# A transformer block with mLSTM, windowed attention and PEER experts: the front half reordered around its modulation, with gated late loads

## The chip, the cores and the metric

The program runs on one core of a Trainium2 chip. The metric is the device time of one execution in microseconds (us); where several executions are shown, their median counts.

## The reference, cut to what is computed

```python
sh1, sc1, g1, sh2, sc2, g2 = split(silu(c) @ w_ada + b_ada, 6)      # 6 x 1024, also for the context
h_lat = rms(x) * norm_mix_g * (1 + sc1) + sh1                      # x: 512 tokens x 1024
h_ctx = ...                                                        # the same for 256 context tokens
p = h @ w_in          # mLSTM q, k, v, o and gates; attention q (8 heads), k, v (2 heads); 2 x 1024 merge gates
m = mlstm(...)        # 4 heads of 128, chunks of 128, forwards and backwards, rms, times sigmoid(o)
a = window_attention(...)  # blocks of 128 queries, keys of 3 blocks and 256 of context, sink, rope
x = x + g1 * ((sigmoid(gm) * (m @ w_bm) + sigmoid(ga) * (a @ w_ba)) @ w_out)
x = x + g2 * peer(rms(x) * norm_ffn_g * (1 + sc2) + sh2)
# peer: 8 heads, 2 x 128 sub keys, top 16 of 16384 experts; gelu(u . h), weighted sum of v; u, v: 16384 x 1024
```

All in float32.

## The kernel before, in words

A product in nearly full precision is made of three matmuls in the `float32r` type (`mm3`): an operand is split into a high part `hi` (an ACT copy) and a low part `lo` (VectorE, DVE, or GpSimd, POOL, subtracts the high part). This is `split`. Weights come in tiles of 512 KB (`wraw`, four buffers), their parts are `whi` and `wlo` (three buffers each). TensorE is called PE, the engine whose queue issues most DMAs SP.

The front, up to 583 us, has these stages. The first half of the modulation's columns that the front needs comes from PE out of `w_ada0`; the rest from DVE `dot`s over a transposed `w_ada`: `late_mod` inside the first projection, `adas` for the 32 columns (`mod[:, 16:48]`) that only the merge and PEER read. `silu` prepares the vector for these dots. `modulated` tokens `xT`, scaled by the root mean square (`rms_rows`), are split to `hhi`, `hlo` and projected with `w_in`. Then come the four mLSTM heads, a preparation of attention's q and k (root mean square, rope, stacking), attention in four blocks `n` of 128 queries with 4, 5, 5 and 4 key blocks, each key block being eight transposes (`PE.transpose(pp...)`), two copies out of PSUM into `pTs` and two products; then a merge with `w_bm` and `w_ba`, `w_out`, and the norm ahead of PEER.

Twenty gate projections (`gate_proj`, 24 matmuls each: four `sigo`, sixteen merge gates, the latter stored in `sgd` and read back in the merge) depend on `hhi` alone. The code writes them after attention, but a list scheduler orders the front's instructions for each engine, and each engine runs its instructions in that order; so gates stand in mLSTM and attention where PE would have nothing else. `ahead(n)` loads tiles of the expert matrix U, makes their low parts and stores them in memory (`lows`); PEER loads them there instead of subtracting. Buffers are reused in a ring, so a load waits until the last reader of its buffer is done. PEER, from 583 us, is written out in an order of its own: query tiles, then streams of U and V tiles, with selection and gathers between.

Before, the loads of `adas` have no other condition than their two buffers (`wada2`), and the scheduler issues them during the projections:

```python
w = wk.tile([128, D], F32, name="wada2", bufs=2)
nc.sync.dma_start(w, A["w_adaT"][j])
dot(w, 0, mod[:, j:j + 1])
```

Of the kernel before, what the change touches and what calls it, by code (L numbers as in the profile page):

```python
# [11 lines left out]
F32 = mybir.dt.float32  # L12
# [16 lines left out]
NH, DH = 4, 128  # L29
# [6 lines left out]
P0, P1 = 10, N1 + 2  # L36


def body(ctx, tc, A, out):
# [147 lines left out]
    for k in range(8):  # L187
        for c in range(2):
            PE.matmul(pm[0:2, c], cc[:, 1, k], wa0[k][:, c], start=(k == 0), stop=(k == 7))
    mrow = [wb([2, 512], F32, "mrow") for _ in range(2)]  # L190
# [6 lines left out]
    pr = rms_rows(acc, T)  # L197
    accc = wk.tile([128, T], F32, name="accc", tag="R", bufs=2)[:, 0:TC]
    for k in range(8):
        square(xcT, k, accc, TC)  # L200
    rc = rms_rows(accc, TC)
    for k in range(8):
        V.tensor_tensor(out=xT[:, k], in0=xT[:, k], in1=pr, op=ALU.mult)
# [8 lines left out]
    for k in range(8):  # L212
        V.tensor_tensor(out=xcT[:, k], in0=xcT[:, k], in1=rc, op=ALU.mult)
# [1179 lines left out]
```

## Time and profile before

| what | value |
|---|---|
| median of three executions | 1848.27 us (1845.07 to 1852.2) |
| the profiled execution | 1850.52 us, its span 1848.7 us |
| mean granted PE clock in it | 0.973 |
| PE, DVE, ACT, POOL busy | 94%, 77%, 41%, 29% of the span |
| bytes moved by DMA | 483.52 MB |
| first mLSTM matmul | 196.3 us |
| first attention score | 311.4 us |
| first merge matmul | 470.0 us |
| first PEER matmul | 583.1 us |

The profile is of one execution; busy shares are averages over stages with different limits, so what an edit is worth has to be read from its own stage.

### The profile page before, as it was taken

The page shows a single profiled execution, that of the slowest core. Times are in us where ns is not written, and L with a number is a line of the kernel's source. Part 1 is how long each engine was busy: PE and PEld are TensorE (multiplying, and loading weights), DVE is VectorE, ACT ScalarE, POOL GpSimd, SP SyncE. Part 2 cuts the span into 40 slices and gives each one's busy share as a digit, 9 for nine tenths or more (in the row PEclk, how much of TensorE's full clock was granted, in tenths as well). Part 3 has the DMA queues.
Part 4 walks back from the last instruction along what each step waited for, and adds up shares of the span by engine and source line. Part 5 has one row for each costly group of instructions (what it writes and reads, how often), then busy time and mean ns, then how long its engine had stood idle before and what let it go on. Part 6 is the DMA issues. An engine that isn't in the chain of part 4 may idle for free.

```text
span 1848.7 us, 25030 instructions
## 1 busy us (share of the span) xinstructions
PE 1741.6 (94%) x9079; PEld 1487.9 (80%) x9079; DVE 1420.8 (77%) x2727; ACT 758.4 (41%) x1126; POOL 529.6 (29%) x422
## 2 busy tenths in 40 slices
PE   6989986998997999999999999999999999999998
PEld 2877875664776889988888999999999999988886
DVE  5858788644654999988828888888888898986665
ACT  5431464655445334544443333333333333333332
POOL 0130154220202554000015454544454454520000
PEclk7999998999998999999989999999999999999999
DMA  8586324545696325699999999999999999987662
GB/s 344 164 282 188 126 86 159 172 145 191 198 305 191 106 90 175 222 323 319 331 310 387 339 352 342 357 344 334 362 327 355 352 331 360 341 335 275 223 213 107
DMA packets 213741, 483.52 MB, mean 262 GB/s; under 512 B 15600, under 2 KB 107248, under 8 KB 212720
## 3 DMA queue, kind: packets, MB, share of 16 engines
q1 hardware_dynamic: 125632, 313.86, 48.1%
q0 software_dynamic: 36864, 134.23, 19.9%
q10 hardware_dynamic: 51120, 33.82, 5.8%
q8 instruction: 71, 1.16, 0.3%
q14 instruction: 54, 0.44, 0.1%
HBM read 419.73 MB, written 62.13 MB: 261 GB/s over the span
## 4 chain that ended last, share of the span: by engine, by line
PE 57%; DMA 8%; DVE 5%; ACT 3%; issue 1%; SPq 1%; ACTq 0%; POOL 0%; DVEq 0%
PE pa L177 9%; PE pa L178 9%; PE pa L176 9%; PE pu L176 9%; PE pu L178 9%; PE pu L177 9%; DMA Gd<-stg 5%; ACT stg L996 1%; DMA wraw<-in_w_out 1%; PE pg L852 1%; PE pg L989 1%; DMA gath<-in_u,idx 1%; DVE pos1h L910 1%; DMA xr<-in_xT 1%; DVE pos1h L899 1%
## 5 line engine op out<-in xcount | busy, mean ns | idle before, releaser
L176 PE MATMUL pu<-h2hi,whi 128*128 128x384 f32 (+1 forms) x1152 | 404.0, 351 | 11.9 <-ACT St L1100 8.3
L178 PE MATMUL pu<-h2lo,whi 128*128 128x384 f32 (+1 forms) x1152 | 396.9, 345 | 0.0
L177 PE MATMUL pu<-h2hi,wlo 128*128 128x384 f32 (+1 forms) x1152 | 396.5, 344 | 0.0
L767 DVE TENSOR_TENSOR wlo<-wraw,whi 128x1024 fp32r<-128x1024 f32 x210 | 256.7, 1223 | 104.4 <-ACT whi L756 102.8
L177 PE MATMUL pa<-whi,wl 128*128 128x512 f32 x768 | 301.3, 392 | 1.5 <-DVE wl L1116 1.4
L176 PE MATMUL pa<-whi,wh 128*128 128x512 f32 x768 | 299.6, 390 | 2.1 <-ACT wh L1112 2.0
L178 PE MATMUL pa<-wlo,wh 128*128 128x512 f32 x768 | 301.1, 392 | 0.0
L756 ACT ACTIVATE whi<-wraw 128x1024 fp32r<-128x1024 f32 x272 | 286.6, 1054 | 27.1 <-PE pa L177 11.8
L1043 POOL DMA_INDIRECT gath<-in_u,idx x128 | 165.1, 1290 | 415.4 <-DMA Sd<-St 241.3
L176 PEld LDWEIGHTS pu<-h2hi,whi 128*128 128x128 f32 x1152 | 219.4, 190 | 22.3 <-ACT St L1100 10.1
L177 PEld LDWEIGHTS pu<-h2hi,wlo 128*128 128x128 f32 x1152 | 219.3, 190 | 7.8
L178 PEld LDWEIGHTS pu<-h2lo,whi 128*128 128x128 f32 x1152 | 218.6, 190 | 5.7 <-DVE h2lo L52 0.6
L1043 POOL DMA_INDIRECT gath<-in_v,idx x128 | 162.0, 1266 | 180.7 <-DVE tokh L1075 164.9
L176 PEld LDWEIGHTS pa<-whi,wh 128*128 128x128 f32 x768 | 144.7, 188 | 31.5 <-ACT wh L1112 3.2
L177 PEld LDWEIGHTS pa<-whi,wl 128*128 128x128 f32 x768 | 144.5, 188 | 31.5 <-DVE wl L1116 2.9
L178 PEld LDWEIGHTS pa<-wlo,wh 128*128 128x128 f32 x768 | 144.4, 188 | 30.0
L1075 DVE SCALAR_TENSOR_TENSOR tokh<-gath,gw,tokh 128x1024 f32<-128x1024 f32 x127 | 162.7, 1281 | 0.6
L1067 DVE CUSTOM_DVE_ANT_0 gath<-gath,tokh 128x1024 f32<-128x1024 f32 x128 | 155.0, 1221 | 5.5 <-DMA gath<-in_u,idx 5.5
L52 POOL TENSOR_TENSOR wlo<-wraw,whi 128x1024 fp32r<-128x1024 f32 (+1 forms) x28 | 71.0, 2538 | 291.1 <-ACT whi L51 232.6
L1112 ACT ACTIVATE wh<-act 128x384 fp32r<-128x384 f32 x84 | 44.2, 526 | 256.8 <-DVE act L1108 254.7
L1100 ACT ACTIVATE act<-pu 128x384 f32<-128x384 f32 x84 | 41.3, 492 | 188.6 <-PE pu L178 188.6
L177 PE MATMUL ps<-hhi,wlo 128*128 128x512 f32 x224 | 93.6, 418 | 11.6 <-POOL wlo L52 11.6
(348 smaller groups left out, 2816.4 us busy)
## 6 DMA issues: line engine op xcount, KB each, us to landing
wraw<-in_uT SPq DMA_DIRECT2D x128, 512.0 KB
wraw<-in_v SPq DMA_DIRECT2D x128, 512.0 KB
Gd<-stg ACTq DMA_DIRECT2D x24, 1024.0 KB
Gt<-Gd SPq DMA_DIRECT2D x32, 768.0 KB
wraw<-in_w_in SPq DMA_DIRECT2D x40, 512.0 KB
sraw<-in_uT SPq DMA_DIRECT2D x36, 512.0 KB
lows<-sraw SPq DMA_DIRECT2D x36, 512.0 KB
wlo<-lows SPq DMA_DIRECT2D x36, 512.0 KB
```

Source lines behind the costliest of these rows:

```text
L52: (eng or V).tensor_tensor(out=lo, in0=src, in1=hi.bitcast(F32), op=ALU.subtract)
L176: PE.matmul(p, sh, mh, start=first, stop=False)
L177: PE.matmul(p, sl, mh, start=False, stop=False)
L178: PE.matmul(p, sh, ml, start=False, stop=last)
L756: S.activation(his[j], raws[j], AF.Copy)
L767: (G if pool else V).tensor_tensor(out=los[j], in0=raws.pop(j), in1=his[j].bitcast(F32), op=ALU.subtract)
L852: PE.matmul(p[:, b], qss[hp][:, b * 128:b * 128 + 128], subk[:, hp], start=True, stop=True)
L1043: G.indirect_dma_start(out=t, out_offset=None, in_=sparse["src"][s // 128], in_offset=bass.IndirectOffsetOnAxis(ap=sparse["idx"][:, s // 1 ...
L1067: V.tensor_tensor_reduce(out=t, in0=t, in1=tokh[:, 0], scale=1.0, scalar=0.0, op0=ALU.mult, op1=ALU.add, accum_out=gw[:, 0, s:s + 1])
L1075: V.scalar_tensor_tensor(out=tokh[:, 1], in0=t, scalar=gw[:, 0, s - 128:s - 127], in1=tokh[:, 1], op0=ALU.mult, op1=ALU.add)
L1100: S.activation(acts[i], p, AF.Gelu_apprx_tanh)
L1112: S.activation(wh, acts[i], AF.Copy)
```

## The change

Eight things change. (1) The first loads are interleaved with those of x, `silu` moves behind the second `w_in` tile, one table load stands early, squares of x are summed two steps before the modulation matmuls end, rows of `xT` are scaled inside the projection loop, and `modulated` writes the high part straight from the scaled row. (2) `adas` takes an argument `now`: the first two tiles of each group are first touched by an ACT copy of one column of `now`, so that their loads wait until that value exists; the groups are one column per mLSTM head, three per attention block, and four in each of the first four merge-gate steps (before: three per head, five per block). (3) The end of the mLSTM (`den` to `num`) becomes `mlstm_end`, behind attention's block 0, without POOL. (4) Other POOL work (squares, rope products, a merge sum, low parts of gate weights) goes to ACT and DVE. (5) Attention's transposes use a double tile `pp2` with two buffers in `a2`. (6) Gate, branch and output weights lie in memory as whole tiles. (7) `ahead` makes tiles 0 to 39 instead of 10 to 45, at other places, and its store goes through POOL's DMA queue right after the subtraction instead of through SP at the next call; in PEER tiles 40 to 45 get their low parts on DVE. (8) In `w_out` the residual rows are loaded two steps ahead.

```diff
-P0, P1 = 10, N1 + 2
+P0, P1 = 0, 40
...
+    for what in (0, 1, "x0", 2, "x1", 3, "x2", 4, "x3", 5, "c", 6, 7):
...
-    silu(0, "c")
-    silu(1, "c_ctx")
-    S.activation(warm, silp[:, 1, 0:1], AF.Sqrt, bias=epsc, scale=0.0)
+    S.activation(warm, cc[:, 1, 0, 0:1], AF.Sqrt, bias=epsc, scale=0.0)
...
-    def adas(a, b):
+    def adas(a, b, now):
...
             w = wk.tile([128, D], F32, name="wada2", bufs=2)
+            if j < a + 2:
+                S.activation(w[:, 0:1], now, AF.Copy)
             nc.sync.dma_start(w, A["w_adaT"][j])
             dot(w, 0, mod[:, j:j + 1])
...
+    def modulated(k, t, a, sh, hi, lo, n, eng=None):
+
+        S.activation(hi[:, k], t, AF.Identity, bias=sh[:, k:k + 1], scale=a[:, k:k + 1])
         h = wb([128, n], F32, "hm")
         S.activation(h, t, AF.Identity, bias=sh[:, k:k + 1], scale=a[:, k:k + 1])
-        split(hi[:, k], lo[:, k], h, eng2)
+        (eng or V).tensor_tensor(out=lo[:, k], in0=h, in1=hi[:, k].bitcast(F32), op=ALU.subtract)
...
     for k in range(8):
+        if k == 6:
+            pr = rms_rows(acc, T)
...
+        if k == 1:
+            silu(0, "c")
+            silu(1, "c_ctx")
...
+        scaled(k + 2)
+        modulated(k, xT[:, k], a1, mod, hhi, hlo, T)
...
     def ahead(n):
-        while made:
-            i, lo = made.pop()
-            nc.sync.dma_start(lows[i - P0], lo)
...
-            made.append((i, raw))
+            nc.gpsimd.dma_start(lows[i - P0], raw)
...
-        adas(16 + 3 * h, 19 + 3 * h)
-    den = wk.tile([128, 2, 4, 4], F32, name="den", bufs=1)
...
+        adas(16 + h, 17 + h, num[1][:, 0, h, 0:1])
...
-            G.tensor_tensor(out=sq, in0=src, in1=src, op=ALU.mult)
+            S.activation(sq, src, AF.Square)
...
-                G.tensor_tensor(out=m2, in0=t, in1=tab[:, w, 1, b][:, None].to_broadcast([128, n, 64]), op=ALU.mult)
+                V.tensor_tensor(out=m2, in0=t, in1=tab[:, w, 1, b][:, None].to_broadcast([128, n, 64]), op=ALU.mult)
...
+    def mlstm_end():
...
+        return hs
...
+            pp2 = pst([128, 2, 4, 128], "a2")
             for g in range(2):
-                pp = pst([128, 4, 128], "a1")
+                pp = pp2[:, g]
...
-        adas(28 + 5 * n, 33 + 5 * n)
+        if n == 0:
+            hs = mlstm_end()
+        ahead(2)
+        adas(20 + 3 * n, 23 + 3 * n, mx[:, 0, 0:1])
...
-        nc.sync.dma_start(gm, A["w_in"][:, col:col + 128].rearrange("(a p) n -> p a n", p=128))
+        nc.sync.dma_start(gm, A["w_gate"][(col - cO) // 128 if col < cX else 4 + (col - cG) // 128])
...
-        split(whi, wlo, gm, G)
+        split(whi, wlo, gm)
...
-        ahead(1)
+        ahead(2)
...
+        if n < 4:
+            adas(32 + 4 * n, 36 + 4 * n, st[:, 0:1])
...
-        for br, nm in ((0, "w_bm"), (1, "w_ba")):
-            nc.sync.dma_start(wbr[:, br], A[nm][:, n * 128:n * 128 + 128].rearrange("(a p) n -> p a n", p=128))
+        nc.sync.dma_start(wbr, A["w_br"][n])
...
-        nc.sync.dma_start(wo, A["w_out"][:, n * 128:n * 128 + 128].rearrange("(a p) n -> p a n", p=128))
+        nc.sync.dma_start(wo, A["w_out"][n])
...
+        if n < 6:
+            load_xr(n + 2)
...
-        ahead(1)
-
-    ahead(0)
...
-            pool = j < 16 + N1
+            pool = j < 16
```

How the order of instructions moves shows at three places. The first is PE at the program's start; `sqa` and `accc` are the summed squares of x and of the context, `wada` and `cc` the modulation's weight and vector. Before:

```order
4 L189 MATMUL ps_151<-wada_105,cc 2x512 x4
5 L196 MATMUL ps<-c_ident,mrow 128x2 x8
6 L159 MATMUL ps<-ones,sqa 128x1 x4
7 L165 MATMUL ps<-c_ident,rr 128x128 x4
8 L159 MATMUL ps<-ones,accc 128x1 x2
9 L165 MATMUL ps<-c_ident,rr 128x128 x2
10 L176 MATMUL ps<-hhi_236,whi 128x512
```

After:

```order
3 L201 MATMUL ps_143<-wada_96,cc 2x512 x4
4 L164 MATMUL ps<-ones,sqa 128x1 x4
5 L170 MATMUL ps<-c_ident,rr 128x128 x4
6 L201 MATMUL ps_143<-wada_97,cc 2x512 x4
7 L211 MATMUL ps<-c_ident,mrow 128x2 x4
8 L164 MATMUL ps<-ones,accc 128x1 x2
9 L211 MATMUL ps<-c_ident,mrow 128x2 x4
10 L170 MATMUL ps<-c_ident,rr 128x128 x2
11 L186 MATMUL ps<-hhi_211,whi 128x512 x4
```

The sums for x moved ahead of the last modulation matmuls, those for the context between the transposes of the result.

The second place is PE in attention's block 2; `sm` are the weights that are transposed, `akv` the values, and matmuls on `hhi` or `hlo` belong to gates. Before:

```order
1368 L178 MATMUL ps<-hlo_238,whi 128x512
1369 L620 MATMUL a_2454<-pTs,akv 64x512
1370 L612 MATMUL a_2572<-c_ident,sm 128x128 x4
1371 L176 MATMUL ps<-hhi_237,whi 128x512
1372 L177 MATMUL ps<-hhi_237,wlo 128x512
1373 L178 MATMUL ps<-hlo_239,whi 128x512
1374 L176 MATMUL ps<-hhi_237,whi 128x512
1375 L612 MATMUL a_2579<-c_ident,sm 128x128 x4
1376 L620 MATMUL a_2454<-pTs,akv 64x512
```

After:

```order
1172 L631 MATMUL a_2561<-c_ident,sm 128x128 x4
1173 L631 MATMUL a_2546<-c_ident,sm 128x128 x4
1174 L639 MATMUL a_2445<-pTs,akv 64x512 x2
1175 L631 MATMUL a_2576<-c_ident,sm 128x128 x4
1176 L631 MATMUL a_2561<-c_ident,sm 128x128 x4
1177 L639 MATMUL a_2445<-pTs,akv 64x512 x2
```

No gate stands there any more, and the transposes for one key block (2576) come before the last four of the block before (2561). Between the first mLSTM matmul and the first of the preparation stand 165 gate matmuls instead of 114, in the preparation 29 instead of 90, from there to the end of attention 46 instead of 276, and behind it 240 instead of none.

The third place is SP while those 240 run; `wada` from `w_adaT` is a column's weights for a dot, `sgd` a gate's store, `sraw` an ahead tile. After:

```order
97 L144 DMA wada_3194<-in_w_adaT 128x1024
98 L144 DMA wada_3198<-in_w_adaT 128x1024
99 L683 DMA sgd<-sgs 128x512
100 L321 DMA sraw<-in_uT 128x1024
101 L144 DMA wada_3202<-in_w_adaT 128x1024
102 L144 DMA wada_3205<-in_w_adaT 128x1024
103 L683 DMA sgd<-sgs 128x512
104 L653 DMA wraw<-in_w_gate 128x1024
105 L144 DMA wada_3288<-in_w_adaT 128x1024
106 L144 DMA wada_3292<-in_w_adaT 128x1024
107 L683 DMA sgd<-sgs 128x512
108 L321 DMA sraw<-in_uT 128x1024
```

These loads stood among those of the projections' weights before:

```order
42 L139 DMA wada_1775<-in_w_adaT 128x1024
43 L265 DMA wraw<-in_w_in 128x2x272
44 L139 DMA wada_1907<-in_w_adaT 128x1024
45 L139 DMA wada_1910<-in_w_adaT 128x1024
46 L265 DMA wraw<-in_w_in 128x2x512
47 L139 DMA wada_1913<-in_w_adaT 128x1024
```

Sixteen of the 32 now stand between attention's end and the last gate weights, and the stores of gates and three gates' weights are queued behind them.

## Rows read from the trace of the kernel before

**Rows 1.** Windows: length, busy PE PEld DVE ACT POOL, clock, DMA share, GB/s.

```profile
0.00:40.00 40.00, 22.94 (x65) 8.32 (x65) 19.07 (x40) 20.04 (x34) 0.20 (x4) 0.81 0.95 374
130.00:196.00 66.00, 59.92 (x272) 47.77 (x272) 49.16 (x114) 16.47 (x23) 4.78 (x2) 0.90 0.62 196
196.00:257.00 61.00, 58.87 (x392) 51.34 (x393) 48.78 (x139) 36.39 (x78) 16.05 (x17) 1.00 0.31 104
257.00:311.00 54.00, 35.89 (x139) 27.01 (x138) 45.99 (x64) 24.17 (x35) 31.07 (x14) 0.82 0.36 118
311.00:444.00 133.00, 127.53 (x574) 83.27 (x572) 72.22 (x163) 79.68 (x131) 28.23 (x11) 1.00 0.52 172
444.00:470.00 26.00, 16.82 (x65) 6.91 (x65) 15.55 (x25) 10.37 (x15) 0.00 (x0) 1.00 0.52 172
470.00:583.00 113.00, 99.15 (x432) 78.89 (x432) 63.05 (x72) 49.10 (x63) 18.51 (x11) 0.95 0.81 256
783.00:960.00 177.00, 161.00 (x1331) 151.96 (x1330) 131.64 (x222) 81.86 (x142) 0.00 (x0) 0.95 0.96 319
```

**Rows 2.** Windows of 10 us, columns as above.

```profile
130.00:140.00 10.00, 8.13 (x32) 6.19 (x32) 7.64 (x20) 4.44 (x7) 0.00 (x0) 0.66 0.87 291
480.00:490.00 10.00, 10.00 (x45) 8.16 (x44) 6.92 (x9) 4.77 (x6) 2.67 (x2) 1.00 0.80 271
570.00:580.00 10.00, 4.77 (x20) 4.31 (x20) 2.27 (x5) 3.34 (x6) 3.56 (x2) 0.55 0.69 232
```

**Rows 3.** ACT in order of time: start, us, instruction, idle before.

```profile
21.41 0.59 ACT L191 ACTIVATE mrow<-ps 2x512 f32<-2x512 f32 x1 [0.35 <-PE ps L189]
...
25.59 1.28 ACT L106 ACT_TABLE_LOAD   x1
...
26.88 2.00 ACT L106 ACTIVATE sig<-sil 128x1024 f32<-128x1024 f32 x2
```

**Rows 4.** PE in order of time.

```profile
36.55 1.01 PE L159 MATMUL ps<-ones,accc 128*128 128x1 f32 x4 [9.25 <-DVE accc L152]
...
39.84 0.79 PE L176 MATMUL ps<-hhi,whi 128*128 128x512 f32 x1 [0.50 <-ACT hhi L51]
```

**Rows 5.** Line 133, the dot: ns min/median/max, first and last start.

```profile
L133 DVE CUSTOM_DVE_ANT_0 wada<-wada,sil x40: 1187/1224/3441, 51.3 to 181.5; 128x1024 f32<-128x1024 f32 x40
```

**Rows 6.** PE's waits before 583: us in total, times, longest.

```profile
PE ps L176 <- DVE gk L327: 5.5, 1, 5.5
...
PE ps L388 <- DVE vL L424: 3.0, 1, 3.0
```

**Rows 7.** Lines 492 and 545, columns as in rows 5.

```profile
L492 DVE TENSOR_TENSOR num<-num,rden x1: 2278/2278/2278, 270.1 to 270.1; 128x2048 f32<-128x2048 f32 x1
...
L545 DVE TENSOR_TENSOR aqt<-aqt,rq x4: 678/680/4083, 258.3 to 289.9; 128x512 f32<-128x512 f32 x4
```

**Rows 8.** Windows from first score and between softmax reciprocals; columns as in rows 1.

```profile
311.40:325.30 13.90, 11.93 (x68) 9.97 (x66) 8.74 (x28) 9.11 (x21) 2.39 (x1) 0.99 0.60 194
...
360.80:402.40 41.60, 41.60 (x185) 26.57 (x184) 20.53 (x46) 24.03 (x38) 7.12 (x3) 1.00 0.45 150
```

**Rows 9.** PE in attention's last block, in order of time.

```profile
457.06 0.66 PE L612 MATMUL a<-c_ident,sm 128*128 128x128 f32 x4 [0.75 <-ACT pTs L617]
...
457.64 1.07 PE L620 MATMUL a<-pTs,akv 128*64 128x512 f32 x2
...
462.00 0.66 PE L612 MATMUL a<-c_ident,sm 128*128 128x128 f32 x4 [0.79 <-DVE pTs L615]
```

**Rows 10.** The chain that ended last, DMAs: start, us, transfer.

```profile
520.89 6.79 DMA wraw<-in_w_out
...
530.11 4.48 DMA sraw<-in_uT
...
540.10 4.95 DMA sraw<-in_uT
```

**Rows 11.** SP's waits: us in total, times, longest.

```profile
SPq L302 <- DMA lows<-sraw: 12.6, 6, 4.0
```

More of the change, by code (lines that the diff above doesn't have):

```diff
@@ L187, in body @@
     for k in range(8):
+        if k == 6:
+            pr = rms_rows(acc, T)
         for c in range(2):
             PE.matmul(pm[0:2, c], cc[:, 1, k], wa0[k][:, c], start=(k == 0), stop=(k == 7))
+    accc = wk.tile([128, T], F32, name="accc", tag="R", bufs=2)[:, 0:TC]
+    for k in range(8):
+        square(xcT, k, accc, TC)
     mrow = [wb([2, 512], F32, "mrow") for _ in range(2)]
@@ L196, in body @@
             PE.transpose(pmc[:, c, k], mrow[c][:, k * 128:k * 128 + 128], ident[0:2, 0:2])
[L197 to L203, printed above, removed]
     for i, m in enumerate((mod, modc)):
@@ L211, in body, with scaled @@
                                op0=ALU.add, op1=ALU.mult)
-    for k in range(8):
-        V.tensor_tensor(out=xcT[:, k], in0=xcT[:, k], in1=rc, op=ALU.mult)
+    rl = wb([128, T], F32, "rl")
+    def scaled(k):
+        if k < 8:
+            V.tensor_tensor(out=xT[:, k], in0=xT[:, k], in1=rl if k else pr, op=ALU.mult)
+    scaled(0)
+    S.activation(rl, pr, AF.Copy)
+    rc = rms_rows(accc, TC)
+    rcs = wb([128, TC], F32, "rcs")
+    S.activation(rcs, rc, AF.Copy)
+    scaled(1)
     pq = [pst([128, T]) for _ in range(6)]
@@ L247, in body @@
             mm3(pq[4 + b], hhi[:, k, sl], hlo[:, k, sl], whi[:, 512:], wlo[:, 512:], k == 0, k == 7)
+    for k in range(8):
+        V.tensor_tensor(out=xcT[:, k], in0=xcT[:, k], in1=rcs, op=ALU.mult)
     for k in range(4, 8):
@@ L569, in body @@
             V.tensor_tensor(out=kst[g][o, 1], in0=pk[a], in1=kst[g][a, 0].bitcast(F32), op=ALU.subtract)
+    def mlstm_end():
+        den = wk.tile([128, 2, 4, 4], F32, name="den", bufs=1)
+        rden = wk.tile([128, 2, 4, 4], F32, name="rden", bufs=1)
+        for d in range(2):
+            S.activation(den[:, d], num[d][:, :, :, 128], AF.Abs)
+            V.tensor_tensor(out=den[:, d], in0=den[:, d], in1=enm[:, :, d], op=ALU.max)
+        V.reciprocal(out=rden, in_=den)
+        for d in range(2):
+            V.tensor_tensor(out=num[d][:, :, :, 0:128], in0=num[d][:, :, :, 0:128],
+                            in1=rden[:, d, :, :, None].to_broadcast([128, 4, 4, 128]), op=ALU.mult)
+        hs = num[0][:, :, :, 0:128]
+        V.tensor_tensor(out=hs, in0=hs, in1=num[1][:, :, :, 0:128], op=ALU.add)
+        sqv = num[1][:, :, :, 0:128]
+        S.activation(sqv, hs, AF.Square)
+        ssq = wk.tile([128, 4, 4], F32, name="ssq", bufs=1)
+        V.tensor_reduce(out=ssq, in_=sqv, op=ALU.add, axis=AX.X)
+        S.activation(ssq, ssq, AF.Sqrt, bias=epsc, scale=1.0 / DH)
+        rs = wk.tile([128, 4, 4], F32, name="rs", bufs=1)
+        V.reciprocal(out=rs, in_=ssq)
+        V.tensor_tensor(out=hs, in0=hs, in1=rs[:, :, :, None].to_broadcast([128, 4, 4, 128]), op=ALU.mult)
+        return hs
     ahi, alo = ga([128, NB, 4, 128], F32R, "ahi"), ga([128, NB, 4, 128], F32R, "alo")
@@ L692, in body @@
         V.tensor_tensor(out=sgs[1], in0=pz[1], in1=sgs[1], op=ALU.mult)
-        G.tensor_tensor(out=z0, in0=sgs[0], in1=sgs[1], op=ALU.add)
+        V.tensor_tensor(out=z0, in0=sgs[0], in1=sgs[1], op=ALU.add)
         split(zh[n // 4][:, n % 4], zl[n // 4][:, n % 4], z0)
```

69 lines of the change are left out of this document (28 added, 41 removed).

## The prediction

> **What bounds the kernel now.** I read the page's slices first: TensorE (PE) is busy nearly everywhere, so time can only come from stretches where PE idles or runs at its lower clock. The windows, cut at milestones of the program, show where these are [rows 1]: before 40 us (22.94 of 40 us busy, and little of that is dense), between the mLSTM and the first attention score at 311 (35.89 of 54), behind attention (16.82 of 26) and from the merge to the first PEER matmul (99.15 of 113). mLSTM and attention are nearly full, because gate-projection matmuls, which depend on nothing late, fill their holes. There are 20 gates of 24 matmuls, 480 in all, and a matmul spaces at 10 us / 45 = 0.222 us [rows 2], so a gate is 5.3 us. Moving gates saves nothing by itself; it only pays where they cover holes.
>
> **The change, by stretch** (milestones of before → after; the counts of gate matmuls are from the order of instructions).
>
> *a. Start: first projection matmul 39.8 → 28.3.* The modulation matmuls are done when their result is copied at 21.41 [rows 3]. From there two table loads (one is shown, 1.28 us), a 2 us silu and a context sum lie in line, so that PE waits 9.25 us for that sum, and the first projection matmul starts at 39.84 [rows 4]. The change takes silu and table loads behind it, starts the squares of x two steps earlier and writes the high part without waiting for hm. Left behind 21.4: the copy 0.59, eight transposes, four small VectorE (DVE) operations, one scaled row, and three ACT copies of 0.6 to 1.1, which I sum to some 7 us, an estimate. Floor 25 (the ACT part alone), ceiling 31 (a table load stays in line). **−11.5.**
>
> *b. First mLSTM matmul 196.3 → 175.8.* The start's −11.5. The 32 later modulation dots (1.22 us each [rows 5]) and their 512 KB loads leave the projections; PE's wait for gk, 5.5 us, is one of DVE standing in such a queue, and goes, as do the 3.0 for vL, and with the clock of 0.66 at 130–140 another 2.5 [rows 2, 6]. Against it stand six ahead subtractions that now come before vL's copy, of which I count 2. **−20.5 in all** (bounds −11 and −24).
>
> *c. mLSTM 60.7 → 76.* 165 gate matmuls instead of 114 between its first matmul and the first preparation transposes. PE's 58.87 busy us [rows 1] less 114 × 0.222 = 25.3 leaves 33.6 of its own; with 165 × 0.222 = 36.6 that is 70.2, and I leave 6 us of holes. **+15.3** (11 to 19).
>
> *d. Preparation of q and k, 54.4 → 36.* Here DVE is the bound: 45.99 busy of 54 [rows 1]. Four passes of the mLSTM end (2.28 as shown, 9.4 in all) leave, and with them the wait for GpSimd's half. The DVE operations beside GpSimd's were stretched (4.08 instead of 0.68 in one row, an excess of 3.4 [rows 7]); for the stretch I estimate 8 us, a little over twice that, which goes with GpSimd's work. Added on DVE: eight products, 4 × 0.68 + 4 × 0.28 = 3.8. 46 − 9.4 − 8 + 3.8 = 32.4, and 3.6 of waits. **−18.4** (−10 if half of the stretching stays, −21).
>
> *e. First score to block 3's reciprocal, 132.5 → 109.* Before, a filled block takes 41.6 us from one softmax reciprocal to the next, with 185 matmuls [rows 8]. After, attention has 46 gate matmuls instead of 276, 12 of them in block 1, none in blocks 2 and 3. What an empty block takes is read from the last one: one key block, four transposes twice and two products, lasts 462.00 − 457.06 = 4.94 us, with PE idle twice for a copy out of the single buffer [rows 9]. Two buffers take these two waits out, which leaves 2 × 0.66 + 2 × 1.07 = 3.5. A block of five is then 9.5 (scores, exponentials; an estimate from the 13.9 us from the first score at 311.4 to the first reciprocal, less fill) + 3.3 for the scaling + 17.5 + about 2.5, because the three dots per block stand between the copies on DVE and their loads, gated on the same reciprocal, land 4.5 to 5 us later [rows 10]: 33 us. 12 + 34 (block 0, with the mLSTM end in it) + 33 + 30 = 109. **−23.5** (−33 to −14).
>
> *f. Block 3's reciprocal to the first merge matmul, 26 → 83.* 240 gate matmuls now follow attention: 17.5 us for four key blocks, 53.3 for the gates, a few for the head transposes: 74 if PE is the bound. It isn't quite: on SP the loads for the 16 last dots stand in two tile buffers, each waiting for the dot two back, and four of them ahead of the weights of each of gates 16 and 17. A pair is a landing of 4.95 and a dot of 1.22 [rows 5, 10], 6.2 us, against 5.3 for a gate. Counted from the reciprocal, dot after dot, the load for gate 15 goes out at 31, for 16 at 44, for 17 at 56; that one lands at 61, is split at 64, and three gates of 5.3 end at 80. With the first merge weights, 83. **+57** (48 to 66).
>
> *g. Merge, w_out, norm, 113.1 → 100.* 384 matmuls are 85 us. Weights in 512-byte rows took 6.79 to land where a contiguous tile of the same size took 4.48 [rows 10], and in w_out the eight ahead tiles with loads and stores are gone; both waits lay on the chain. Left are 11 us of norm and 4 of seams. **−13** (−6 to −16).
>
> *h. PEER −4.* From 783 to 960 the DMA engines are busy 0.96 and PE 161 of 177 us [rows 1]. Forty instead of 36 low parts come from memory, but the first ten of them fall where queues are light; in this stretch there are six tiles fewer, 3 MB, and six more subtractions of 1.22 on DVE, which has 45 us free there. At 319 GB/s 3 MB are 9.8 us; I take under half (0 to −10).
>
> Costed at nothing: the stores of low parts from GpSimd's software queue instead of SP (SP waits up to 4.0 us for such a store to leave its buffer [rows 11]; nobody reads the low parts before 720 us; with a software queue three times slower the ring of four buffers would delay only ahead tiles); the squares on ACT (busy 24 of 54 us there); subtractions for gates on DVE instead of GpSimd.
>
> Sum: −20.5 + 15.3 − 18.4 − 23.5 + 57 − 13 − 4 = −7.1. The profiled execution took 1850.5, its median sibling 1848.3; 1848.3 − 7.1 = **1841 us**.
>
> **Clock.** While PE was busy 16.8 of 26 us behind attention its granted clock stayed at 1.00, full speed; while it was busy 4.77 of 10 us at 570–580 it fell to 0.55 [rows 1, 2], nearly the lower level of 1.2 GHz. Emptied blocks are of the first kind, and the sum has no loss for them. The Trainium skill ("TensorE: Matmul & The Clock Gate", section "HAM oscillation — how this bites in real kernels") says that an engine that waits between bursts drops to its lower clock and starts each burst slow; by that rule attention would lose what rival 3 has, 1865, and the trace so far agrees only at the starved places.
>
> **Rivals.**
> 1. *The gated dots pace everything* (slower). Place: SP from block 3 on. If each load lands in 6.79 instead of 4.95, as the slow ones in w_out do [rows 10], a pair is 8.0 us, eight pairs cost 15 more, and stores of gate results behind them 5: **1861**. It decides from the point where a pair exceeds a gate's 5.3 us by over 2. For it: two buffers, in-order SP and DVE. Against: DMA has only 0.52 share before 470 [rows 1].
> 2. *PE is the bound of the tail and empty blocks are short* (faster): the loads run ahead, −9 in f, and blocks of 30, −6 in e: **1826**. For it: dots are 1.2 us and loads could be in flight early.
> 3. *Emptied attention loses the clock* (slower). PE's own work there is about 60 us in blocks 1 to 3; at 0.66, as in 130–140, with half of it hidden behind DVE, 24: **1865**.
> 4. *The start's gain is swallowed* (slower or same): six ahead tiles take the weight buffers and DVE before vL's copy, and the mLSTM starts no earlier than 196; of 20.5 lost nothing is given back: **1861**. For it: each such tile keeps its buffer until its store is out [rows 11]. Against: the projections are fully paced by PE.
>
> **Chances.** Forecast 0.42 (its own range 1830 to 1853), rival 1 0.15, rival 2 0.25, rival 3 0.08, rival 4 0.10. A measurement of this kernel tells some 0.5%, 9 us, from no change: under 1839 is faster, over 1857.5 slower. Faster: rival 2 nearly whole and under half of the forecast, 0.42. Same: half of the forecast and edges, 0.30. Slower: most of 1, 3, 4, 0.28. Leaving out a tenth on either side gives 1813 to 1866.
>
> **What would show it.** First projection matmul near 28, first mLSTM matmul near 176, first score near 288, block reciprocals 33 us apart, first merge matmul near 480, first PEER matmul near 580. A first mLSTM matmul after 190, blocks over 38 us, PE idle over 10 us between attention and merge, or a granted clock under 0.8 in attention would each break a step.

## The result

The changed kernel takes 1895.18 us (median of four, 1892.56 to 1899.37) where the kernel before takes 1850.24 (median of four measured beside it): slower by a ratio of 1.0244, 95% interval 1.0207 to 1.0282. The forecast was 1841, with 1830 to 1853 as its own range.

The profiled execution has a span of 1894.3 us and a mean granted clock of 0.959 instead of 0.973. Its windows, cut at the same milestones as [rows 1] (length, busy time of PE, PEld, DVE, ACT and POOL, granted clock, DMA share, GB/s):

```profile
0.00:28.60 28.60, 21.06 (x65) 6.43 (x65) 11.79 (x30) 13.66 (x28) 0.20 (x4) 0.99 0.93 365
28.60:179.90 151.30, 142.29 (x705) 117.50 (x705) 85.56 (x174) 66.39 (x96) 25.44 (x23) 0.97 0.47 157
179.90:264.00 84.10, 76.22 (x456) 66.26 (x457) 66.25 (x163) 58.55 (x113) 9.28 (x16) 0.95 0.69 238
264.00:290.80 26.80, 14.98 (x66) 10.54 (x65) 25.36 (x62) 13.49 (x21) 0.53 (x1) 0.75 0.32 118
290.80:416.20 125.40, 92.08 (x342) 49.70 (x342) 85.14 (x185) 51.33 (x104) 2.13 (x4) 0.82 0.27 97
416.20:509.00 92.80, 78.09 (x304) 54.87 (x304) 56.24 (x80) 34.09 (x51) 4.80 (x9) 0.91 0.82 278
509.00:625.70 116.70, 101.58 (x432) 81.49 (x432) 63.46 (x72) 40.79 (x54) 10.87 (x10) 0.91 0.64 209
```

They are the start, the projections, the mLSTM, the preparation, attention up to block 3's reciprocal, the stretch from there to the first merge matmul, and merge to norm. Against the kernel before:

| stretch | before | forecast | measured | miss |
|---|---|---|---|---|
| a, start | 39.8 | 28.3 | 28.6 | 0 |
| b, to the first mLSTM matmul | 196.3 | 175.8 | 179.9 | +4 |
| c, mLSTM | 60.7 | 76 | 84.1 | +8 |
| d, preparation | 54.4 | 36 | 26.8 | −9 |
| e, first score to block 3's reciprocal | 132.5 | 109 | 125.4 | +16 |
| f, from there to the first merge matmul | 26.1 | 83 | 92.8 | +10 |
| g, merge, w_out, norm | 113.1 | 100 | 116.7 | +17 |
| h, PEER | 1265.6 | 1261.6 | 1268.6 | +7 |

The start came out as forecast. The loss sits in f, which is 66.7 us longer, and in e, which gives only 7.1 of it back. In the windows above, PE is busy 92.08 of 125.40 us in attention at a granted clock of 0.82, where it was busy 127.53 of 133 at 1.00 before: attention was emptied of matmuls and hardly got shorter.

Where SP stood shows in its timeline (start, length, instruction; L144 loads a dot's column, L653 a gate's weights, L683 stores a gate):

```profile
347.40 0.80 SPq L144 DMA_DIRECT2D wada<-in_w_adaT  x2
348.29 0.38 SPq L653 DMA_DIRECT2D wraw<-in_w_gate  x1
352.94 79.82 SPq L144 DMA_DIRECT2D wada<-in_w_adaT  x10
432.85 0.38 SPq L683 DMA_DIRECT2D sgd<-sgs  x1
```

From 352.94 to 432.76 SP issues ten dot loads and nothing else. Its waits over the run (total, times, longest) name what these loads waited for, the one-column ACT copies, and a second thing, the ahead tiles' stores, which held the buffers of the next ahead loads (L321):

```profile
SPq L144 <- ACT wada L143: 83.2, 12, 29.8
SPq L321 <- DMA lows<-sraw: 79.5, 14, 15.3
```

### The profile page after: what moved, and what is told of

Its sections match the earlier page's. It is cut to its first block, busy times and chain, and to the rows that moved or that the text cites. A ratio compares the mean times of both kernels' runs of the same rounds, so it can differ in the third digit from the quotient of the medians.

```text
span 1894.3 us, 25043 instructions
## 1 busy us (share of the span) xinstructions
PE 1757.0 (93%) x9079; PEld 1495.6 (79%) x9079; DVE 1438.6 (76%) x2774; ACT 764.6 (40%) x1155; POOL 433.5 (23%) x404
## 4 chain that ended last, share of the span: by engine, by line
PE 64%; issue 15%; DMA 9%; DVE 5%; ACT 4%; POOL 1%; ACTq 1%; SPq 0%; POOLq 0%; DVEq 0%
PE pa L187 9%; PE pa L188 9%; PE pa L186 9%; PE pu L186 9%; PE pu L188 9%; PE pu L187 9%; DMA Gd<-stg 5%; PE ps L186 2%; PE ps L187 2%; PE ps L188 2%; ACT stg L1026 2%; DMA lows<-sraw 1%; DMA sraw<-in_uT 1%; ACT whi L786 1%; PE pg L882 1%
## 5 line engine op out<-in xcount | busy, mean ns | idle before, releaser
L797 DVE TENSOR_TENSOR wlo<-wraw,whi 128x1024 fp32r<-128x1024 f32 x216 | 264.3, 1223 | 141.6 <-ACT whi L786 139.2
L1073 POOL DMA_INDIRECT gath<-in_u,idx x128 | 160.6, 1255 | 437.0 <-DMA Sd<-St 256.9
L1073 POOL DMA_INDIRECT gath<-in_v,idx x128 | 167.6, 1309 | 179.6 <-DVE tokh L1105 164.2
L325 POOL DMA_DIRECT2D lows<-sraw x40 | 21.6, 540 | 412.8 <-DVE sraw L324 330.7
L52 DVE TENSOR_TENSOR wlo<-wraw,whi 128x1024 fp32r<-128x1024 f32 x52 | 63.5, 1221 | 55.1 <-ACT whi L51 54.9
```

Of the source, the lines that this page charges most:

```text
L52: (eng or V).tensor_tensor(out=lo, in0=src, in1=hi.bitcast(F32), op=ALU.subtract)
L797: (G if pool else V).tensor_tensor(out=los[j], in0=raws.pop(j), in1=his[j].bitcast(F32), op=ALU.subtract)
L1073: G.indirect_dma_start(out=t, out_offset=None, in_=sparse["src"][s // 128], in_offset=bass.IndirectOffsetOnAxis(ap=sparse["idx"][:, s // 1 ...
```

## Experiments

Each comparison is with runs of the kernel before on the same chip, whose medians were 1854.5, 1854.4, 1854.0 and 1850.9 in the four groups (runs 1 to 4, 5 to 8, 9 to 12, 13 to 15). The changed kernel was measured once, beside a kernel before at 1850.2, so a difference to it carries some 4 us of doubt. Windows are of one profiled execution each. Three theories were stated: G, the gated dots make the loss; S, the ahead tiles' stores through GpSimd's queue do; D, the work that left GpSimd overloads DVE.

**1. The changed kernel, dots ungated.**

```diff
-    def adas(a, b, now):
+    def adas(a, b):
...
-            if j < a + 2:
-                S.activation(w[:, 0:1], now, AF.Copy)
...
-        adas(20 + 3 * n, 23 + 3 * n, mx[:, 0, 0:1])
+        adas(28 + 5 * n, 33 + 5 * n)
...
-        if n < 4:
-            adas(32 + 4 * n, 36 + 4 * n, st[:, 0:1])
```

> The changed kernel with one part undone: the later modulation dots are as before, three per head and five per block, and their loads wait for nothing but their buffers. In the order of instructions 245 gate matmuls then stand in attention and 63 behind it, where the changed kernel has 47 and 239. Theory G (the gated dots make the loss: they empty attention and pace the tail): attention to first merge matmul, 218 us in the changed kernel, falls to about 165, total 1845 to 1855. Theory S (the ahead tiles' stores through the software queue hold the four weight buffers): the tail and the merge stay as slow, total 1880 to 1890. Theory D (work moved from GpSimd overloads VectorE): 1885 to 1895.

Measured 1846.36 us, 0.9961 (0.9933 to 0.9988) of before: 49 us less than the changed kernel. From the first score to block 3's reciprocal 128.1, from there to the merge 33.9; the projections are 14 us longer, as the dots are back in them. G holds.

**2. The kernel before, dots gated.** The same edit the other way on the kernel before, nothing else.

> The kernel before with one part of the change alone: the gated dots in their new groups. 60 gate matmuls stand in attention and 225 behind it, instead of 276 and none. Theory G: 1875 to 1890, with first merge matmul 30 us later than before. Theories S and D: 1845 to 1855, since stores and GpSimd's work are as before.

Measured 1913.16 us, 1.0317 (1.0251 to 1.0383): this part alone costs 59 us, where the whole change costs 45 (the two intervals overlap). Its windows for e and f:

```profile
298.60:435.00 136.40, 103.38 (x342) 49.96 (x340) 72.15 (x174) 48.55 (x102) 9.49 (x4) 0.78 0.30 100
435.00:529.70 94.70, 75.66 (x305) 52.99 (x305) 51.99 (x71) 31.48 (x49) 16.72 (x7) 0.90 0.80 258
```

Attention takes 136.4 us with 342 matmuls in it and the stretch behind it 94.7. More than G gave, in the same place.

**3. The changed kernel, ahead tiles as before.**

```diff
-P0, P1 = 0, 40
+P0, P1 = 10, N1 + 2
...
-            nc.gpsimd.dma_start(lows[i - P0], raw)
+            made.append((i, raw))
```

> The changed kernel with the ahead tiles as before: tiles 10 to 45, one at a time at the old places, stores by SP at the next call. Theory S: waits of SP for stores go, the mLSTM starts at 175, merge and w_out take 100 us instead of 117, total 1860 to 1870. Theory G: 1885 to 1895.

Measured 1865.56 us, 1.0067 (1.0035 to 1.0099): 30 us less than the changed kernel, so the ahead tiles cost as well, beside G. Whether it is their stores' queue, as S has it, or their number and place, this run does not separate; run 6 does. The mLSTM:

```profile
176.30:244.30 68.00, 67.99 (x440) 59.53 (x441) 55.05 (x151) 48.31 (x101) 2.87 (x4) 1.00 0.41 148
```

It takes 68.0 us with PE busy throughout, where the changed kernel had 84.1 with 76.22 busy; the first mLSTM matmul is at 176.3, and w_out with the norm takes 61.6 instead of 68.2. The stretch behind attention, 93.7, is untouched: the two losses are apart.

**4. The changed kernel, GpSimd's work back on it.**

```diff
-            S.activation(sq, src, AF.Square)
+            G.tensor_tensor(out=sq, in0=src, in1=src, op=ALU.mult)
...
-        split(whi, wlo, gm)
+        split(whi, wlo, gm, G)
```

The rope product, the merge sum and the mLSTM's end went back in the same way.

> The changed kernel with GpSimd's work back on GpSimd and the mLSTM's end ahead of the preparation as before. Theory D: VectorE is freed, total 1875 to 1885. Theories G and S: the preparation takes 45 to 55 us again instead of 27, partly given back by the matmuls that then lie in it (72 instead of 29), total 1895 to 1910.

Measured 1913.75 us, 1.0329 (1.0272 to 1.0385), 19 us more than the changed kernel and a little over what G and S gave. The preparation takes 48.4 us:

```profile
265.20:313.60 48.40, 30.01 (x118) 22.50 (x117) 47.41 (x60) 19.16 (x28) 26.90 (x16) 0.82 0.28 93
```

DVE is busy 47.41 of them. D falls: taking GpSimd's work away, together with the mLSTM's end, is a gain.

**5. The changed kernel, the last dots gated on attention's last block.** Two theories for f were left: P, the forecast's own, that the pairs of loads pace the gates, and H, that a gate's result is held.

```diff
-            adas(32 + 4 * n, 36 + 4 * n, st[:, 0:1])
+            adas(32 + 4 * n, 36 + 4 * n, alo[:, 3, 0, 0:1].bitcast(F32))
```

> The changed kernel with one thing other: the last 16 dots wait for a column of attention's last block instead of for the gates' result tiles. Their loads come no earlier and are as many. Theory H (hold): the copy that reads a gate's result keeps that one of two result buffers until a dot's tile is free, which is after attention's last block; so only ten of twenty gates could stand ahead of that. In the order of instructions 248 gate matmuls are then in attention and 38 behind it. By it the stretch from block 3's reciprocal to the first merge matmul falls from 93 to 35 to 45 us, attention from first score to that reciprocal goes from 125 to 130 to 145, total 1850 to 1870. Theory P (the pairs of loads pace the gates, as the forecast had it): the loads stand behind attention as before, and that stretch stays over 75 us, total over 1880.

Measured 1850.87 us, 0.9991 (0.9967 to 1.0015): 44 us less than the changed kernel by one argument. Attention, the stretch behind it, and the merge up to w_out:

```profile
288.20:418.60 130.40, 118.22 (x512) 77.15 (x513) 96.52 (x195) 75.51 (x132) 4.78 (x9) 0.92 0.49 169
418.60:450.70 32.10, 31.32 (x136) 19.05 (x134) 25.59 (x38) 16.93 (x27) 2.13 (x4) 1.00 0.79 265
450.70:516.00 65.30, 50.05 (x192) 38.34 (x193) 51.46 (x74) 21.10 (x29) 3.72 (x7) 0.90 0.93 335
```

f is 32.1 us. Attention takes 130.4 us with 512 matmuls in it, 5 us more than with 342: the gates lay there almost for nothing. The 16 loads and dots now lie in the merge, which takes 65.3 instead of 48.5. The first of these loads goes out 22.9 us behind the reciprocal, in the changed kernel 9.4. Behind the reciprocal 70 gate matmuls are left instead of 240, so the run tests why gates stand there and not what paces those that do.

How a gate is held shows in the changed kernel's ACT timeline (L143 is the one-column copy, L660 a gate's sigmoid with its table load):

```profile
425.38 0.19 ACT L143 ACTIVATE wada<-sgs 128x1 f32<-128x1 f32 x1
...
429.65 0.19 ACT L143 ACTIVATE wada<-sgs 128x1 f32<-128x1 f32 x1
...
430.36 1.28 ACT L660 ACT_TABLE_LOAD   x1
431.65 0.60 ACT L660 ACTIVATE sgs<-ps 128x512 f32<-128x512 f32 x1
...
443.72 0.20 ACT L143 ACTIVATE wada<-sgs 128x1 f32<-128x1 f32 x1 [0.37 <-DVE mod L135]
444.86 0.20 ACT L143 ACTIVATE wada<-sgs 128x1 f32<-128x1 f32 x1 [0.94 <-DVE mod L135]
445.10 0.60 ACT L660 ACTIVATE sgs<-ps 128x512 f32<-128x512 f32 x1
```

The first two copies that read a gate's result (`wada<-sgs`) run at 425.38 and 429.65, each right after a dot of attention's last block left a dot tile (DVE, L135):

```profile
423.13 1.22 DVE L135 CUSTOM_DVE_ANT_0 wada<-wada,sil 128x1024 f32<-128x1024 f32 x1
...
427.91 1.22 DVE L135 CUSTOM_DVE_ANT_0 wada<-wada,sil 128x1024 f32<-128x1024 f32 x1
```

Sigmoids of gates, taken from the same timeline, stand at 198.4, 215.4, 228.3 and 236.5 (`sigo`), 256.1, 260.5, 268.0 and 273.8 (merge gates), and then not before 431.65:

```profile
273.80 0.60 ACT L660 ACTIVATE sgs<-ps 128x512 f32<-128x512 f32 x1 [2.20 <-PE ps L188]
```

The second and the fourth merge gate are the last of their step, so their results are what the copies read. Each step has two copies, one for each dot tile; by this order the copies at 425.38 and 429.65 end the hold on the second gate's result, and those at 443.72 and 444.86 that on the fourth's, and a sigmoid follows each pair. From 273.80 to 431.65, 158 us, no gate gets a result buffer. Eight gates with a sigmoid and two more whose sums stay in PSUM, where gates have two banks, make ten gates, 240 matmuls, as many as the order of instructions had ahead of this point, and as many as the trace has between the first mLSTM matmul and 431.65. Runs 2 and 3, which have the same copies, also have 240 behind the reciprocal.

**6. The changed kernel, stores by SP.**

```diff
-            nc.gpsimd.dma_start(lows[i - P0], raw)
+            nc.sync.dma_start(lows[i - P0], raw)
```

> The changed kernel with the 40 ahead stores issued by SP, right behind the subtraction, instead of by GpSimd. Theory Q (the software queue's slow stores keep the weight buffers): the mLSTM takes 70 us instead of 84, w_out 62 instead of 68, total 1870 to 1880. Theory N (it is how many tiles come early, whoever stores them, and SP now waits for each subtraction): the mLSTM stays at 80 or more, total 1890 to 1905.

Measured 1874.82 us, 1.0124 (1.0077 to 1.0171), 20 us less than the changed kernel. The mLSTM, and w_out with the norm, in this run, and the latter in the changed kernel:

```profile
177.30:252.60 75.30, 71.12 (x446) 61.15 (x447) 66.47 (x163) 58.26 (x112) 2.84 (x4) 1.00 0.78 267
545.80:605.10 59.30, 52.62 (x240) 43.12 (x240) 29.26 (x30) 20.95 (x31) 7.13 (x3) 0.93 0.50 165
```

```profile
557.50:625.70 68.20, 55.22 (x241) 44.27 (x239) 31.27 (x34) 20.56 (x32) 7.14 (x3) 0.87 0.47 150
```

Of the 16 us that the ahead tiles cost the mLSTM, the queue accounts for 9 (84.1 to 75.3) and their number and place for 7 (75.3 to 68.0); in w_out the queue accounts for 9 (68.2 to 59.3). On the chain that ended last (start, us, transfer), a store in the changed kernel's merge, and one in this run's:

```profile
533.15 6.89 DMA lows<-sraw
...
555.25 6.70 DMA lows<-sraw
```

```profile
526.27 2.91 DMA lows<-sraw
```

6.7 to 6.9 us against 2.9. These are few: on the chains of the merge in all runs, stores through GpSimd's queue took 4.0 to 9.0 us (eleven, median 7.0) and those through SP's 2.8 to 6.4 (eight, median 2.9). With the store the weight ring's buffer comes free, and with that the next weights: behind the store at 555.25 SP issues a load of `w_out` and then one of a stored gate, and PE waits 7.3 us at the start of `w_out` for the split of the merge's last result, a wait that this run does not have. The forecast had costed this edit at nothing, because nobody reads the low parts before 720 us and a slow queue would delay only ahead tiles. But gate, branch and output weights use the same four buffers; what it costs is the buffer, not the result.

**7. Both parts undone.** The changed kernel without gated dots and with the ahead tiles as before; start, layout, GpSimd's work, mLSTM's end and double tile stay.

> The changed kernel with both the gated dots and the ahead tiles as before. If the two losses are apart: from ungated, 1846, the 16 us of the mLSTM, 4 ahead of it and 7 of w_out go: 1815 to 1825, faster than before by 1.5%. If the early ahead tiles only filled time that the ungated dots take anyway: 1835 to 1846.

Measured 1817.22 us, 0.9798 (0.975 to 0.9846): the fastest of all, 37 us under before. Attention and the stretch behind it:

```profile
276.80:404.00 127.20, 117.61 (x512) 75.94 (x512) 87.83 (x178) 75.60 (x126) 0.00 (x0) 0.95 0.40 138
404.00:443.30 39.30, 38.65 (x171) 25.83 (x169) 23.92 (x32) 19.85 (x27) 0.00 (x0) 1.00 0.62 207
```

**8. As 7, with dots gated as in 5.**

> As the run before it, but with the dots gated, the last 16 on attention's last block. Gated dots leave the projections (about 14 us there) and no gate is held: theory H gives 1805 to 1825. If the dots cost as much in attention as in the projections: the same as the run before it within 6 us. Theory P: 1850 or more.

Measured 1830.91 us, 0.989 (0.984 to 0.9939), 14 us more than 7, between what H and P gave. The gated dots gain 11 us in the projections (147.7 instead of 158.8 us) and lose 21 in the merge (71.1 instead of 49.8), where the last 16 and their loads lie.

**9. The kernel before, with the weights laid out whole and early residual rows.**

```diff
-        nc.sync.dma_start(wo, A["w_out"][:, n * 128:n * 128 + 128].rearrange("(a p) n -> p a n", p=128))
+        nc.sync.dma_start(wo, A["w_out"][n])
...
+        if n < 6:
+            load_xr(n + 2)
```

> The kernel before with two parts alone: gate, branch and output weights laid out whole, residual rows of w_out loaded two ahead. The order of gate matmuls is that of before. As forecast, merge to first PEER matmul takes 102 to 107 us instead of 113, total 6 to 11 us less. Rival: weights were hidden and the stage is held by ahead tiles and loads of gates anyway: within 3 us of before.

Measured 1850.75 us, 0.9987 (0.996 to 1.0014): 3 us under the runs of before beside it, no change that can be told. Merge, and w_out with the norm, in the kernel before and here:

```profile
470.00:515.10 45.10, 44.66 (x192) 35.79 (x193) 28.43 (x34) 17.97 (x21) 10.47 (x7) 1.00 0.70 230
515.10:583.10 68.00, 54.49 (x241) 43.10 (x241) 34.64 (x40) 31.23 (x42) 8.14 (x5) 0.91 0.89 273
```

```profile
472.90:518.20 45.30, 44.65 (x192) 35.81 (x192) 28.71 (x34) 18.00 (x21) 10.91 (x7) 1.00 0.65 225
518.20:582.40 64.20, 52.92 (x241) 41.19 (x240) 35.96 (x39) 31.42 (x42) 9.43 (x5) 0.96 0.88 291
```

In the merge PE is busy 44.66 of 45.1 us in the kernel before: nothing was left to gain there. W_out with the norm is 3.8 us shorter in the one profile.

**10. As 7, with single-buffered transposes.**

```diff
-            pp2 = pst([128, 2, 4, 128], "a2")
...
-                pp = pp2[:, g]
+                pp = pst([128, 4, 128], "a1")
```

> The seventh run's kernel with attention's transposes as before, one buffer of one bank for each half. In the order 315 gate matmuls stand in attention and 6 behind it. If the double tile shortens key blocks on the path: 8 to 15 us slower than the seventh run. If gates fill the gaps anyway: within 4 us.

Measured 1819.59 us, 0.982 (0.9779 to 0.9862), 2 us from run 7. The second branch: blocks last 38 to 41 us instead of 33 to 38, and the stretch behind attention takes 29.6 instead of 39.3, since more gates found room.

**11. The kernel before, with the new start.** Its edit is the first part of the diff above, up to `modulated`.

> The kernel before with the new start alone. First projection matmul at 28 to 29 instead of 39.8. If the gain lasts: total 9 to 12 us less. If later waits take it back (the ungated dots' loads come at the same times): under 5 us less.

Measured 1854.09 us, 0.9989 (0.996 to 1.0018). The first projection matmul is at 29.1, 10.7 us earlier, and the first mLSTM matmul at 192.1, 4.2 earlier: with ungated dots the projections give 6.5 us back. PE's wait for gk, which [rows 6] had at 5.5, is still there (total, times, longest):

```profile
PE ps L183 <- DVE gk L344: 6.2, 1, 6.2
PE ps L405 <- DVE vL L441: 2.7, 1, 2.7
```

The rest goes behind attention, which takes 34.9 us to the merge instead of 26.1.

**12. As 7, all dots gated evenly.**

```diff
+            if j < a + 2:
+                S.activation(w[:, 0:1], now, AF.Copy)
...
+        adas(16 + 3 * h, 19 + 3 * h, num[1][:, 0, h, 0:1])
...
+        adas(28 + 5 * n, 33 + 5 * n, mx[:, 0, 0:1])
```

> The seventh run's kernel with all 32 dots gated in the groups of before: three per head on the head's result, five per block on the block's reciprocals, none behind attention, so that no gate's result is read. 212 gate matmuls stand in the mLSTM, 235 in attention, none behind. If gated dots only need to hold nothing: projections 11 us shorter, mLSTM 15 longer for its 72 more matmuls, which the tail gives back: 1800 to 1815. If dots behind their loads stall VectorE in the blocks: 1820 to 1835.

Measured 1832.32 us, 0.9881 (0.9839 to 0.9923), the second branch by its time, and not by its place: projections 11.5 us shorter than in 7, mLSTM 85.8 instead of 63.3, preparation 30.1 instead of 25.6, attention 141.9 instead of 127.2, the stretch behind it 23.9 instead of 39.3. How much of attention's 15 us are dots that wait for their loads was not taken apart.

**13. The changed kernel with PE kept busy ahead of the transposes.**

```diff
+        if n:
+            dump = pst([128, 4, 128], "a1")
+            for h in (6, 6, 7, 7):
+                PE.matmul(dump.rearrange("p a b -> p (a b)"), ident, Pp[h][:, 0:512], start=True, stop=True)
```

> The changed kernel with four additional matmuls in blocks 1 to 3 that read two finished heads' weights and whose result nobody uses; they lie between a block's scores and its transposes, where PE waits 4 to 5.5 us for the scaling. If the lower clock behind that wait holds the block: granted clock near 1.00 from 340 to 420, the first two key blocks at 4.3 us instead of 5, blocks 30 to 31 us instead of 34 to 36, total 8 to 12 us less. If the chain of scores, exponentials, scaling and copies holds it: blocks 34 to 36, total within 4 us.

Measured 1891.95 us, 1.0225 (1.0169 to 1.0282), 3 us under the changed kernel and not to be told from it. From block 1's reciprocal to block 2's and on to block 3's, in the changed kernel and here:

```profile
346.90:382.50 35.60, 27.11 (x92) 12.41 (x92) 19.17 (x48) 11.02 (x25) 0.00 (x0) 0.83 0.21 77
382.50:416.20 33.70, 25.51 (x92) 11.81 (x92) 18.09 (x47) 10.22 (x25) 0.00 (x0) 0.85 0.14 47
```

```profile
342.80:374.80 32.00, 25.35 (x98) 11.79 (x97) 19.16 (x47) 11.02 (x25) 0.00 (x0) 0.97 0.24 85
374.80:409.10 34.30, 28.12 (x102) 12.85 (x101) 18.09 (x47) 10.21 (x25) 0.00 (x0) 0.93 0.14 47
```

The granted clock rises from 0.83 and 0.85 to 0.97 and 0.93, and the two blocks together take 66.3 us instead of 69.3, one 3.6 shorter and the other 0.6 longer. So the clock holds little of it. That the chain of scores, exponentials, scaling and copies holds the rest is the other branch, argued from what is left.

**14. The changed kernel without attention's dots.**

```diff
-        adas(20 + 3 * n, 23 + 3 * n, mx[:, 0, 0:1])
+        if n == 3:
+            V.memset(mod[:, 20:32], 0.0)
```

> The changed kernel without the twelve dots of attention's blocks (twelve columns of the modulation are zero, 6 MB fewer are loaded); the last 16 dots still wait for gates' result tiles. 220 gate matmuls stand in attention in the order and 67 behind it. Theory H: with nothing of attention in the two dot tiles, gates are held no longer, block 3 to merge falls from 93 to 40 to 55, total 1845 to 1860. Theory P: the last 16 dots pace the gates, over 75, total over 1880.

Measured 1845.61 us, 0.9964 (0.9936 to 0.9993). The stretch from block 3's reciprocal to the merge:

```profile
428.00:464.70 36.70, 36.01 (x159) 23.38 (x157) 22.78 (x31) 18.24 (x25) 2.13 (x4) 1.00 0.57 199
```

36.7 us, while the last 16 dots wait for gates' results as in the changed kernel. Attention takes 135.4 us instead of 125.4, with 491 matmuls instead of 342. H holds from the other side: results are held only when the dot tiles are still wanted by attention. The last 16 loads are all out by 398.5, ahead of the reciprocal at 428, so pairs of loads behind attention are not tested here.

**15. The kernel before, GpSimd's work off and mLSTM's end moved.** The reverse of 4, on the kernel before.

> The kernel before with two parts alone: GpSimd's work to ACT and VectorE, and the mLSTM's end behind attention's block 0. 19 gate matmuls stand in the preparation instead of 90. The fourth run with this undone was 19 us slower than the changed kernel, so: preparation 25 to 30 us instead of 54, mLSTM 6 longer, attention 5 to 10 longer, total 1825 to 1838. Rival: the gates that leave the preparation come back elsewhere, total within 5 us of before.

Measured 1825.07 us, 0.986 (0.9806 to 0.9914): of the parts tried alone (runs 2, 9, 11 and 15) the one that gains, 26 us. GpSimd's work and the place of the mLSTM's end were not taken apart. Its preparation, and the rope line that answers to L545 in [rows 7] (min/median/max ns):

```profile
259.70:285.70 26.00, 15.99 (x67) 11.64 (x66) 24.19 (x61) 12.94 (x21) 0.00 (x0) 0.74 0.30 101
```

```profile
L525 DVE TENSOR_TENSOR aqt<-aqt,rq x4: 679/683/686, 261.0 to 274.5; 128x512 f32<-128x512 f32 x4
```

26.0 us instead of 54.4; no instruction of that line takes over 686 ns where one took 4083 with GpSimd busy beside it for 3.54 us.

## Why the prediction was wrong

Two steps failed. The larger is the edit that was costed at nothing, the ahead tiles with their stores. Of the 53 us that the stretches of the table miss together, b, c, g and h hold 36, and run 3, which takes that edit out, is 30 us faster, by the two profiled executions 36: 4 in b, 16 in c, 7.5 in g and 9 in h. That the two sums agree so well is in part luck: in run 3 g is still 9 us over its forecast, and c 8 under. The other step is e with f: the forecast let an emptied attention give back 23.5 us of the 57 that its gates cost behind it; it gave 7.1, against 66.7. That is a miss of 26 us, of which d, cut at the same border as e, takes 9 back. The gated dots are still the larger part of the loss itself: runs 1, 2 and 5 put them at 44 to 59 us, and for these the forecast had the 57 of f.

*f.* The path was right and sized 10 us short: 83 us were forecast, 92.8 measured. 240 matmuls did follow attention, and the weights of the last gates did stand on SP behind pairs of dot loads:

```profile
452.79 0.38 SPq L653 DMA_DIRECT2D wraw<-in_w_gate  x1
...
466.60 0.55 SPq L653 DMA_DIRECT2D wraw<-in_w_gate  x1
...
480.00 0.38 SPq L653 DMA_DIRECT2D wraw<-in_w_gate  x1
```

Counted from the reciprocal at 416.2 that is 36.6, 50.4 and 63.8 us, where the forecast had 31, 44 and 56; two pairs take 13.4 to 13.8, so a pair some 6.8 instead of 6.2. PE is idle 14.7 us in this stretch, the one of the four signs of a broken step that came. What the forecast took as given from the order is that 240 gate matmuls have to follow at all. A copy that reads a gate's result into a dot tile ties the gates' two result buffers to attention's last dots. The forecast gave this copy no cost and asked for the queue of loads behind it, not for what its source has to wait for. Without the hold the stretch takes 32.1 us (run 5) and 36.7 (run 14).

*e.* The forecast took a filled block of 41.6 us for one that gates lengthen. In run 5 attention has 512 matmuls recorded where the changed kernel has 342, and pays 5 us for the 170 more, 37.7 by 0.222 each; run 14 pays 10 for 149, run 1 2.7 for 181. So with the double tile in place, emptying a block gave 1.7 to 3.4 us on the mean, not the 8.6 between 41.6 and 33. An empty block was sized nearly right, 33 us forecast and 34.0, 35.6 and 33.7 measured between reciprocals, but a key block takes 4.3 us, not 3.5: the wait for DVE's copy stays. PE in block 1 of the changed kernel:

```profile
363.01 1.07 PE L639 MATMUL a<-pTs,akv 128*64 128x512 f32 x2
364.94 1.07 PE L639 MATMUL a<-pTs,akv 128*64 128x512 f32 x2 [0.85 <-DVE pTs L634]
365.94 1.41 PE L631 MATMUL a<-c_ident,sm 128*128 128x128 f32 x8
```

Two products, 0.85 us of waiting, two products, eight transposes: 365.94 + 1.41 − 363.01 = 4.3. The first key blocks are slower, after PE stood 5.53 us:

```profile
347.87 1.99 PE L631 MATMUL a<-c_ident,sm 128*128 128x128 f32 x8 [5.53 <-DVE sm L624]
...
351.16 1.97 PE L639 MATMUL a<-pTs,akv 128*64 128x512 f32 x2
...
354.39 1.97 PE L639 MATMUL a<-pTs,akv 128*64 128x512 f32 x2 [0.85 <-DVE pTs L634]
```

Products take 1.97 instead of 1.07 here, at a granted clock of 0.50 (347.87 to 356.29), the lower level of 1.2 GHz. The sum had no loss for the clock, and rival 3 had this with 24 us; run 13 raises the clock to 0.97 and 0.93 and gains 3. The Trainium skill ("TensorE: Matmul & The Clock Gate", section "HAM oscillation — how this bites in real kernels") says that bursts after waits start slow; these rows agree. By run 13 it makes little of the loss.

The larger part of e's miss, 10 of 16 us, is a border: scores began before the preparation was over, so that d was 9 us shorter and the first reciprocal 22.2 us behind the first score instead of 12. From the mLSTM's end to that reciprocal 48 us were forecast and 48.9 measured.

*c, b.* Both are the ahead tiles: in run 3 the mLSTM's first matmul is at 176.3, half a microsecond from the forecast, and the mLSTM takes 68.0, so that the tiles cost 16 us there, where 6 us of holes were allowed in all. That edit was costed at nothing, and run 6 puts 9 of the 16 down to the queue that stores; that the eight tiles made beside the mLSTM's first gates hold weight buffers is argued for the rest. Rival 4 named those buffers, but wanted 20 us of it ahead of the mLSTM.

*g.* Two terms, both wrong. The layout gives nothing in the merge and nothing that can be told in the total (run 9), although [rows 10] had transfers of 6.79 and 4.48 us in the chain. In the kernel before PE waits 4.0 us for low parts of weights in the whole of g, and 9.5 for the norm's sums and its result, so faster weights had no 13 us to gain: a transfer on the chain that ended last is not worth its whole length when PE hardly waits for it. And the stores through GpSimd's queue cost 9 us in w_out (run 6).

*h.* In run 3 PEER takes 8.9 us less than in the changed kernel. All profiled runs of the changed kernel with the old ahead tiles (3, 7, 8, 10, 12) have 1259.0 to 1261.9 us, those with the new ones (1, 4, 5, 6, 13, 14) 1264.4 to 1267.9, so the new tiles cost some 3 to 9 there; the 3 MB fewer gave nothing that shows. Why was not taken further.

*d* was right in kind: 26.8 us instead of 36, of which the border of e is a part. Run 15 shows it alone, and as the change's real gain, 26.0. DVE is busy 25.36 us in it where 32.4 were forecast. The 8 us taken for the stretching beside GpSimd were too few: six groups of rope instructions that took 21.1 us before take 9.8 after, 11.3 less. The rest is mainly ahead subtractions that have left the window, 1.2 us of them instead of 4.9.

*a* was right, 28.6 for 28.3. Run 11 shows that an earlier start isn't by itself an earlier end: 6.5 of its 10.7 us are lost in projections that hold the ungated dots, and runs 7 and 8 put what these dots cost there at 11.

Rival 1 was nearest in direction and named the place where f overshot, pairs of loads longer than 6.2 us; it gave 1861, and 15 us of the loss to that.

## What to carry to other kernels

When a copy is added only to delay something, look at both of its ends: its source stays held until its target is free, so a ring of two results can be tied to a ring of two scratch tiles far away. Matmuls that fill another engine's chain cost little there (5 us for 37.7 us of them in run 5), so an order that empties a chain has to be charged the whole of what it moves. And cost a store by the buffer that it keeps, not by who reads its result.

## What the runs showed of the hardware

On the chains that ended last, the ahead stores of 512 KB in the merge took 4.0 to 9.0 us through GpSimd's queue (changed kernel, runs 1, 4, 5, 13 and 14) and 2.8 to 6.4 through SP's (runs 3, 6, 7, 10, 12 and 15). A product of DVE that takes 0.68 us took 4.08 with GpSimd busy beside it, and in run 15, without GpSimd's products, none of its line took over 0.69. A granted clock raised from 0.83 and 0.85 to 0.97 and 0.93 by idle matmuls moved two blocks by 3 us of 69.
